# A gate read out of PSUM by ScalarE instead of VectorE, in a hybrid decoder step

## The chip, the cores and the metric

The kernel runs on one core of a Trainium2 chip. The metric is the device time of one launch in microseconds. The trace is one execution recorded by the hardware profiler; its times count from the first instruction. PE is TensorE's matmul row and PEld its weight loads, DVE is VectorE, ACT is ScalarE, POOL is GpSimd, and SP is the engine that issues most transfers. A tile is called by its name in the program.

## What is computed

One layer of a decoder with three branches that share one input projection, over a prompt of 1024 tokens and 8 single-token samples (1032 columns together, model width 1024):

```
h    = RMSNorm(x);  proj = h @ w_in          # split into 11 parts
A: dilated window attention, 12 heads of 64   * silu(z_A)   # 768 channels
B: u * (tril(W_s) @ LayerNorm(v) + b)         * silu(z_B)   # 512 channels
C: gated linear recurrence, 6 heads of 128    * silu(z_C)   # 768 channels, its q is silu(q_pre)
y    = x + concat(A, B, C) @ w_out
```

`silu(z) = z / (1 + exp(-z))`. The parts z_A, z_B, z_C and q_pre, 2816 channels in all, go through the function that is changed. All data are fp32; the large products are made of three passes over operands split into a high and a low part.

## The kernel before

`attention()` goes through three pairs of head pairs: projections of q, k, v and of z_A, then the attention of each head. `hgrn()` goes through three pairs of heads of branch C. For each pair it projects the values (`c_proj_i`, PSUM tile `pi`, and for the samples `pss_ci`). For each head it projects q and the forget gate (`c_proj_qf`, tile `pc`), runs the recurrence in chunks (`levels` and `c_head`: tiles `T` on DVE and ACT, products `lv`, `ls`, `po` on PE), the samples' step (`c_step`) and one head pair's attention of the samples over the cache (`decode`, with the small products `pmb` and `pda`, and `dmb` on DVE). Between the two heads stands the projection of z_C (`c_proj_z`, tile `pcz`). `sgu()` is branch B, with z_B in `pbz`. `out_proj` ends the program.

A transposed projection writes 128 channels by a third of the 1032 columns (344) at a time: 24 matmuls into one PSUM tile of tag `proj`, of which there are two. The tile is free again when its last reader is done. All projections, the natural ones too, take turns on these two tiles.

`gate(dst, ps, nm)` follows each such chunk of z or q. It runs 66 times: 18 for z_A, 18 for q, 18 for z_C, 12 for z_B. L152 reads PSUM on DVE and writes `max(ps, -43)` to `dst` in SBUF, L153 to L155 are three ACT instructions over the temporary `t`, and L156 multiplies on DVE. The temporary has tag `gt`, with two buffers; in `c_proj_qf` the forget gate's tile `ft` (written at L581 and last read at L582, both DVE) takes the same two buffers. The forget gate itself already goes from PSUM through ACT at L572, and L575 bounds its exponential in SBUF on DVE:

```
nc.scalar.activation(kk[:, cs], ps[:, :TC], AF.Exp, scale=-1.0)   # L572
nc.vector.tensor_scalar(kk, kk, 2.0 ** 62, None, ALU.min)         # L575
```

Weights come by transfer into `raw` tiles; ACT makes the high part (L192) and POOL the low part (L193) of each. The order of the instructions on each engine isn't written by hand: a planner (`schedule_with_timeline_sim=True`) takes the program's order as priority and its own table of costs, and lays the queues out. Each engine then works through its queue in order.

Of the kernel before, what the change touches and what calls it, by code (L numbers as in the profile page):

```python
# [12 lines left out]
AF = mybir.ActivationFunctionType  # L13
ALU = mybir.AluOpType
# [24 lines left out]
RUNS = ((0, 1, 3), (3, 3, 1), (4, 2, 2))  # L39
NEG = -3.0e38  # L40
BIG = 3.0e38
LIM = 43.0
N_BIG, N_S2, N_S2B, N_PQ, N_W, N_WL, N_GT, N_RAW, N_E = 16, 6, 2, 5, 4, 4, 2, 6, 3


# [46 lines left out]
def hybrid_step(tc, ins, outs, parts=("A", "D", "B", "C", "O"), dbg=None):  # L92
    nc = tc.nc
# [8 lines left out]
    with tc.tile_pool(name="const", bufs=1) as cp, tc.tile_pool(name="sb", bufs=1) as sb, \  # L102
# [20 lines left out]
        def small(nm, n, p=P, dt=F32, bufs=2, tag=None):  # L123
            return sb.tile([p, n], dt, tag=tag or f"sm{n}", name=nm, bufs=bufs)
# [10 lines left out]
        def p_st(nm):  # L135
            return psum("st", nm, 4)
# [12 lines left out]
        def gate(dst, ps, nm):  # L149

            t = small(nm, TC, tag="gt", bufs=N_GT)
            nc.vector.tensor_scalar(dst, ps, -LIM, None, ALU.max)  # L152
            nc.scalar.activation(t, dst, AF.Exp, scale=-1.0)  # L153
            nc.scalar.activation(t, t, AF.Ln, bias=1.0)
            nc.scalar.activation(t, t, AF.Exp, scale=-1.0)  # L155
            nc.vector.tensor_tensor(dst, dst, t, ALU.mult)  # L156
# [49 lines left out]
        for t in (0, NT, *range(1, NT)):  # L206
# [7 lines left out]
            if t == NT:  # L214
                nc.vector.tensor_tensor_reduce(out=xn[:n, :], in0=xt[:n, :], in1=xt[:n, :], op0=ALU.mult, op1=ALU.add,
                                               scale=1.0, scalar=0.0, accum_out=ss[:n, 0:1])
# [9 lines left out]
            for j in range(2):  # L226
                ps = p_st(f"tr0_{t}_{j}").rearrange("p (a b) -> p a b", a=4)
# [151 lines left out]
        def az_proj(sp):  # L379
            blk = load_w([(OFF_AZ + sp * NW, NW)], f"az{sp}")  # L380
            Z = [inp(f"az{sp}_{j}") for j in range(2)]
            for j in range(2):
                for c in range(3):
                    ps = p_proj(f"paz{sp}_{j}_{c}")
                    proj_T(blk, j * P, c, ps[:, :TC])
                    gate(Z[j][:, c * TC:(c + 1) * TC], ps[:, :TC], f"azt{sp}_{j}_{c}")
                nc.scalar.copy(ysT[:, 2 * sp + j, :], Z[j][:, S:L])
            return Z
# [172 lines left out]
        def c_proj_qf(h):  # L561
            blk = load_w([(OFF_CQ + h * P, P), (OFF_CF + h * P, P)], f"cqf{h}")
            f, q, kk = inp(f"f{h}"), inp(f"q{h}"), inp(f"k{h}")
            for j, dst in ((1, kk), (0, q)):
                for c in range(3):
                    ps = p_proj(f"pc{h}_{j}_{c}")
                    proj_T(blk, j * P, c, ps[:, :TC])
                    cs = slice(c * TC, (c + 1) * TC)
                    if j == 0:
                        gate(q[:, cs], ps[:, :TC], f"qt{h}_{c}")  # L570
                    else:
                        nc.scalar.activation(kk[:, cs], ps[:, :TC], AF.Exp, scale=-1.0)  # L572
                if j == 1:

                    nc.vector.tensor_scalar(kk, kk, 2.0 ** 62, None, ALU.min)  # L575
                    nc.scalar.activation(f, kk, AF.Ln, bias=1.0)
                    nc.scalar.activation(f, f, AF.Exp, scale=-1.0)
                    for c in range(3):
                        cs = slice(c * TC, (c + 1) * TC)
                        t = small(f"ft{h}_{c}", TC, tag="gt", bufs=N_GT)  # L580
                        nc.vector.scalar_tensor_tensor(t, kk[:, cs], 1.0, f[:, cs], ALU.add, ALU.mult)  # L581
                        nc.vector.scalar_tensor_tensor(f[:, cs], t, 2.0, f[:, cs], ALU.subtract, ALU.mult)  # L582
            nc.vector.scalar_tensor_tensor(kk, kk, lb1[:, h:h + 1], f, ALU.mult, ALU.mult)
            nc.scalar.activation(f, f, AF.Identity, scale=lb1[:, h:h + 1], bias=lb[:, h:h + 1])
            qw = small(f"qs{h}", 5 * NS, tag="qs", bufs=2)
            nc.gpsimd.memset(qw[:, 3 * NS:], 0.0)
            qs = qw[:, 0:3 * NS].rearrange("p (a b) -> p a b", a=3)
            for i, x in enumerate((q, f, kk)):
                nc.scalar.copy(qs[:, i, :], x[:, S:L])
            return q, f, kk, qw  # L590
# [14 lines left out]
        def c_proj_z(hp):  # L605
            blk = load_w([(OFF_CZ + hp * NW, NW)], f"cz{hp}")
            Z = [inp(f"cz{hp}_{j}") for j in range(2)]
            for j in range(2):
                for c in range(3):
                    ps = p_proj(f"pcz{hp}_{j}_{c}")  # L610
                    proj_T(blk, j * P, c, ps[:, :TC])
                    gate(Z[j][:, c * TC:(c + 1) * TC], ps[:, :TC], f"czt{hp}_{j}_{c}")
            for j in range(2):
                nc.scalar.copy(zsT[:, 2 * hp + j, :], Z[j][:, S:L])
            return Z
# [463 lines left out]
```

## Time and profile before

| | us |
|---|---|
| median of 3 runs | 1289.98 |
| lowest and highest of them | 1288.97, 1293.23 |
| the profiled execution, device time | 1287.74 |
| its span, first to last instruction | 1286.0 |
| what lies around the span | 1.74 |

The mean granted TensorE clock of the span is 0.977 of full speed. The stages, by the span: attention up to about 475, branch C from there to about 975 with the first projections of branch B inside its end, branch B to about 1065, and the output projection to the end. PE, DVE and ACT work on neighbouring stages at once, since the planner fills one stage's gaps with the next one's projections.

### The profile page before, as it was taken

The numbers are of one execution on the slowest core, as the hardware profiler recorded it, in microseconds if no ns is written. First come the engines' busy times: TensorE is split into PE (matmuls) and PEld (weight loads), VectorE is DVE, ScalarE is ACT, GpSimd is POOL, SyncE is SP. The second block draws the span as 40 slices with busy tenths as digits, with TensorE's granted clock in tenths as the row PEclk, the third lists the DMA queues.
The fourth block names the chain that finished last, engine by engine and source line by source line (L and its number), as shares of the span: only waits on it lengthen the run. The fifth ranks groups of instructions, "written<-read, shape, count | busy, mean of one in ns | idle before, by whom it ended". The sixth has DMA issues, their size and how long they took to land.

```text
span 1286.0 us, 27698 instructions
## 1 busy us (share of the span) xinstructions
PE 1215.2 (94%) x10610; PEld 1129.3 (88%) x10610; DVE 916.5 (71%) x2427; ACT 644.2 (50%) x1486; POOL 285.5 (22%) x272
## 2 busy tenths in 40 slices
PE   4899989999999999998999989997999999999998
PEld 3899979999899988997888878887889899899998
DVE  5844778668776685879888897889796534664643
ACT  4444444745347554565445554565443242454543
POOL 3532112312123121121011111111011254122221
PEclk9999989999899999999999989999899999999999
DMA  6151032312223123124343424424353224621110
GB/s 234 24 148 54 14 105 62 111 51 59 57 78 107 38 84 89 29 64 107 91 134 96 117 61 134 132 66 106 95 153 95 86 68 134 203 79 46 62 47 29
DMA packets 165045, 114.17 MB, mean 89 GB/s; under 512 B 13945, under 2 KB 158993, under 8 KB 164913
## 3 DMA queue, kind: packets, MB, share of 16 engines
q1 hardware_dynamic: 157520, 110.28, 29.4%
q10 hardware_dynamic: 6816, 1.54, 0.6%
q8 instruction: 83, 1.36, 0.5%
q0 software_dynamic: 576, 0.58, 0.3%
q14 instruction: 50, 0.40, 0.1%
HBM read 84.47 MB, written 22.09 MB: 83 GB/s over the span
## 4 chain that ended last, share of the span: by engine, by line
PE 75%; DVE 15%; DMA 4%; issue 3%; ACT 2%; SPq 0%; POOL 0%; ACTq 0%; DVEq 0%; POOLq 0%
PE po L100 15%; PE pqk L100 10%; PE pv L100 9%; PE paz L100 5%; PE pi L100 5%; PE st L100 4%; PE pbu L100 4%; PE pc L100 4%; PE pbz L100 4%; PE pbv L100 3%; PE pcz L100 2%; PE s L100 2%; DMA dk<-in_cache_k_dram 2%; DVE T L628 2%; DVE T L630 1%
## 5 line engine op out<-in xcount | busy, mean ns | idle before, releaser
L100 PE MATMUL pqk<-wh_qk,h 128*128 128x256 f32 x768 | 157.4, 294 | 5.8 <-ACT h L233 3.0
L100 PE MATMUL pc<-h,wh_cqf 128*128 128x344 f32 x576 | 141.6, 326 | 11.3 <-DVE cz L152 8.0
L100 PE MATMUL po<-woh,yh 128*128 128x256 f32 x512 | 144.1, 282 | 0.5 <-ACT yh L1027 0.5
L100 PE MATMUL po<-woh,yl 128*128 128x256 f32 x512 | 144.2, 282 | 0.0
L100 PE MATMUL po<-wol,yh 128*128 128x256 f32 x512 | 143.4, 280 | 0.0
L100 PEld LDWEIGHTS pqk<-wh_qk,h 128*128 128x128 f32 x768 | 127.8, 197 | 12.3 <-ACT h L233 4.3
L100 PE MATMUL pqk<-wl_qk,h 128*128 128x256 f32 x384 | 113.0, 294 | 0.0
L100 PEld LDWEIGHTS pc<-h,wh_cqf 128*128 128x128 f32 x576 | 100.4, 190 | 14.0 <-DVE cz L152 8.8
L100 PEld LDWEIGHTS po<-woh,yl 128*128 128x128 f32 x512 | 96.2, 188 | 3.0 <-issue 1.7
L100 PEld LDWEIGHTS po<-woh,yh 128*128 128x128 f32 x512 | 96.3, 188 | 2.3 <-ACT yh L1027 2.3
L100 PEld LDWEIGHTS po<-wol,yh 128*128 128x128 f32 x512 | 96.5, 188 | 0.0
L437 DVE CUSTOM_DVE_ANT_0 s<-s,masks 128x512 f32<-128x512 f32 (+2 forms) x144 | 77.6, 578 | 22.7 <-PE s L100 21.7
L100 PE MATMUL pc<-h,wl_cqf 128*128 128x344 f32 x288 | 93.7, 327 | 0.0
L100 PE MATMUL pi<-wh_ci,h 128*128 128x256 f32 x384 | 77.5, 295 | 0.8 <-DVE T L635 0.8
L100 PEld LDWEIGHTS pqk<-wl_qk,h 128*128 128x128 f32 x384 | 75.9, 198 | 1.8 <-issue 0.7
L100 PE MATMUL pv<-wh_v,h 128*128 128x256 f32 x384 | 75.3, 287 | 0.3 <-DVE ss L164 0.3
L100 PE MATMUL pcz<-h,wh_cz 128*128 128x344 f32 x288 | 72.2, 330 | 2.3 <-DVE q L152 2.3
L100 PE MATMUL paz<-h,wh_az 128*128 128x344 f32 x288 | 69.0, 323 | 0.0
L1028 DVE TENSOR_TENSOR yl<-yb,yh 128x512 fp32r<-128x512 f32 x44 | 30.3, 691 | 53.3 <-ACT yh L1027 53.3
L100 PEld LDWEIGHTS pi<-wh_ci,h 128*128 128x128 f32 x384 | 63.5, 198 | 2.7 <-issue 2.4
L100 PEld LDWEIGHTS pv<-wh_v,h 128*128 128x128 f32 x384 | 61.8, 193 | 1.9 <-issue 1.2
L1027 ACT CAST yh<-yb 128x512 fp32r<-128x512 f32 x64 | 39.6, 620 | 43.4 <-PE po L100 43.4
(379 smaller groups left out, 3581.6 us busy)
## 6 DMA issues: line engine op xcount, KB each, us to landing
wro<-in_w_out_dram SPq DMA_DIRECT2D x32, 256.0 KB
wr_qk<-in_w_in_dram SPq DMA_DIRECT2D x48, 128.0 KB
wr_cqf<-in_w_in_dram SPq DMA_DIRECT2D x48, 128.0 KB
dk<-in_cache_k_dram SPq DMA_DIRECT2D x24, 192.0 KB
dv<-in_cache_v_dram SPq DMA_DIRECT2D x24, 192.0 KB
xt<-in_x_prompt_dram SPq DMA_DIRECT2D x8, 512.0 KB
xr<-in_x_prompt_dram SPq DMA_DIRECT2D x32, 128.0 KB
out_o_yp_dram<-xr SPq DMA_DIRECT2D x32, 128.0 KB
```

What stands on the lines that cost most here:

```text
L100: nc.tensor.matmul(out, lhsT=lhsT, rhs=rhs, start=start, stop=stop)
L437: nc.vector.tensor_tensor_reduce(out=ps[:, :w], in0=ps[:, :w], in1=nmask[:, S - n + c:S - n + c + w], op0=ALU.add, op1=ALU.max, scale=1.0, ...
L628: nc.vector.tensor_tensor(K.rearrange("p (n w) -> p n w", w=w), g3[:, :, w - 1:w].to_broadcast([P, 4 * n, w]), h3, ALU.subtract)
L630: nc.vector.tensor_tensor(Q[:, 0:3], g4[:, 1:4], g4[:, 0:3, :, w - 1:w].to_broadcast([P, 3, n, w]), ALU.subtract)
L1027: nc.scalar.copy(yh[:, sl, :], y)
L1028: (nc.gpsimd if piece == 0 else nc.vector).tensor_tensor(yl[:, sl, :], y, yh[:, sl, :].bitcast(F32), ALU.subtract)
```

## The change

The gate no longer reads PSUM on DVE. ACT takes the exponential of the negated argument straight from PSUM into the temporary, and copies the unbounded argument from PSUM to `dst`. DVE bounds the exponential in SBUF at 2 to the power 62, in place. The logarithm, the second exponential and the product stay. The function is called at the same four places, 66 times.

```diff
@@ -39,7 +39,6 @@
 BIG = 3.0e38
-LIM = 43.0
 N_BIG, N_S2, N_S2B, N_PQ, N_W, N_WL, N_GT, N_RAW, N_E = 16, 6, 2, 5, 4, 4, 2, 6, 3
@@ -149,8 +148,9 @@
             t = small(nm, TC, tag="gt", bufs=N_GT)
-            nc.vector.tensor_scalar(dst, ps, -LIM, None, ALU.max)
-            nc.scalar.activation(t, dst, AF.Exp, scale=-1.0)
+            nc.scalar.activation(t, ps, AF.Exp, scale=-1.0)
+            nc.scalar.copy(dst, ps)
+            nc.vector.tensor_scalar(t, t, 2.0 ** 62, None, ALU.min)
             nc.scalar.activation(t, t, AF.Ln, bias=1.0)
             nc.scalar.activation(t, t, AF.Exp, scale=-1.0)
             nc.vector.tensor_tensor(dst, dst, t, ALU.mult)
```

## Rows read from the trace of the kernel before

**Rows 1.** The page, part 1: busy us (share of the span) and instructions of each engine.
```profile
PE 1215.2 (94%) x10610; PEld 1129.3 (88%) x10610; DVE 916.5 (71%) x2427; ACT 644.2 (50%) x1486; POOL 285.5 (22%) x272
```

**Rows 2.** The page, part 4: the chain that ended last, share of the span by engine.
```profile
PE 75%; DVE 15%; DMA 4%; issue 3%; ACT 2%; SPq 0%; POOL 0%; ACTq 0%; DVEq 0%; POOLq 0%
```

**Rows 3.** Windows: length, then each engine's busy us (instructions), granted clock, DMA share, GB/s.
```profile
247.00:278.00 31.00, 31.00 (x211) 29.32 (x210) 18.98 (x51) 20.10 (x44) 14.44 (x18) 1.00 0.33 97
...
530.00:975.00 445.00, 413.82 (x4355) 378.39 (x4354) 382.88 (x1076) 238.63 (x564) 73.68 (x68) 0.97 0.37 102
...
975.00:1065.00 90.00, 90.00 (x746) 83.52 (x745) 48.93 (x136) 34.84 (x80) 30.64 (x24) 1.00 0.30 90
...
755.00:760.00 5.00, 3.76 (x25) 2.27 (x18) 4.94 (x16) 4.38 (x9) 1.49 (x1) 0.50 0.48 138
```

**Rows 4.** Waits of PE from 530 to 975: us in total, times, longest.
```profile
PE pc L100 <- DVE cz L152: 8.0, 3, 3.0
...
PE pss_ci L100 <- DVE q L152: 4.3, 2, 3.7
...
PE pss_bv L100 <- DVE q L152: 3.7, 1, 3.7
...
PE pcz L100 <- DVE q L152: 2.3, 2, 1.8
...
PE pc L100 <- DVE q L152: 0.9, 2, 0.5
...
PE pc L100 <- ACT V L602: 2.5, 2, 2.2
...
PE pmb L941 <- DVE dmb L939: 5.0, 3, 3.4
```

**Rows 5.** Instructions of four lines: duration in ns (min/median/max), first and last start.
```profile
L152 DVE TENSOR_SCALAR q<-pc x18: 496/501/517, 532.8 to 900.2; 128x344 f32<-128x344 f32 x18
...
L572 ACT ACTIVATE k<-pc x18: 444/458/461, 512.5 to 879.2; 128x344 f32<-128x344 f32 x18
...
L575 DVE TENSOR_SCALAR k<-k x6: 682/687/699, 524.9 to 882.7; 128x1032 f32<-128x1032 f32 x6
...
L939 DVE COPY dmb<-dmb x6: 207/215/1199, 612.8 to 960.3; 16x128 f32<-16x128 f32 x6
```

**Rows 6.** Timeline, 742 to 758: start, duration (us), what [idle before <-releaser].
```profile
742.66 0.51 DVE L152 TENSOR_SCALAR q<-pc 128x344 f32<-128x344 f32 x1
...
745.45 0.49 ACT L153 ACTIVATE qt<-q 128x344 f32<-128x344 f32 x1 [2.39 <-DVE f L582]
...
754.27 0.50 DVE L152 TENSOR_SCALAR q<-pc 128x344 f32<-128x344 f32 x1
...
754.81 0.49 ACT L153 ACTIVATE qt<-q 128x344 f32<-128x344 f32 x1 [2.91 <-DVE q L152]
...
754.83 1.89 PE L100 MATMUL pss_ci<-wr_ci,hs 128*8 128x256 f32 x16 [3.68 <-DVE q L152]
...
755.88 1.49 POOL L193 TENSOR_TENSOR wl_ci<-wr_ci,wh_ci 128x512 fp32r<-128x512 f32 x1 [1.75 <-ACT wh_ci L192]
...
756.25 1.20 DVE L939 COPY dmb<-dmb 16x128 f32<-16x128 f32 x1
...
757.50 0.29 PE L941 MATMUL pmb<-ident,dmb 16*128 16x16 f32 x1 [0.78 <-DVE dmb L939]
```

**Rows 7.** Timeline, 606 to 609.
```profile
606.36 6.45 POOL L193 TENSOR_TENSOR wl_ci<-wr_ci,wh_ci 128x512 fp32r<-128x512 f32 x4 [27.47 <-ACT wh_ci L192]
...
608.05 0.50 DVE L152 TENSOR_SCALAR q<-pc 128x344 f32<-128x344 f32 x1
```

**Rows 8.** Timeline of PE, 727 to 732.
```profile
727.39 0.58 PE L100 MATMUL pc<-h,wh_cqf 128*128 128x344 f32 x2 [3.02 <-DVE cz L152]
...
731.59 0.25 PE L100 MATMUL lv<-T 128*32 128x32 f32 x2
```

**Rows 9.** Window 530 to 975, line L193 alone: POOL busy us (instructions), then clock and DMA.
```profile
530.00:975.00 445.00, 70.84 (x51) 0.97 0.37 102
```

## The prediction

> **What bounds the kernel now.** I first read the page's busy times: PE is busy 94% of the span, DVE 71%, ACT 50% [rows 1]. The chain of waits is three quarters PE and 15% DVE, and only 2% ACT [rows 2]. So the kernel is bound by PE, and a change on DVE and ACT can move the end only through PE's idle time. The windows say where that is. Beside the gates of z_A and z_B, PE is busy in all of 31.00 us and in all of 90.00 us. In the stage of branch C it is busy for 413.8 of 445 us, so it idles for 31.2 us, while DVE is busy for 86% of that stage and ACT for 54% [rows 3]. Next I read PE's waits in this stage: five rows name L152, the gate's reading of PSUM on DVE. They sum to 8.0 + 4.3 + 3.7 + 2.3 + 0.9 = 19.2 us [rows 4]. In these PE waits for one of the two projection tiles, because DVE is late in emptying it. Where ACT empties the tile, PE waited 2.5 us in all.
>
> One such place shows how it comes about. ACT idles 2.91 us and PE 3.68 us for the same L152, which stands at 754.27 in a full DVE queue [rows 6]; in 755 to 760 DVE is busy 4.94 of 5 us and the granted clock after the gap is 0.50, the level of 1.2 GHz [rows 3]. Then PE waits again, for `dmb`, which also comes from DVE [rows 6].
>
> **The change part by part.** It issues no transfer, and moves none past another: only three instructions of each gate change. Of 66 gates, the 30 of z_A and z_B I cost at nothing: the cover is PE's unbroken work there [rows 3], against which ACT's addition is small. If that cover were gone, 30 copies of 0.46 us would cost 13.7 us. What follows is for the 36 gates of branch C.
>
> *DVE's work.* A maximum from PSUM of 0.501 us goes, and a minimum in SBUF comes. L575 is the same operation on 1032 columns, 0.687 us; a copy in SBUF of 128 columns takes 0.215 [rows 5]. The line between them gives 0.33 us at 344 columns; 0.215 and 0.501 bound it. So 0.17 us is saved each, 36 x 0.17 = 6.2 us. That counts only where DVE is late. I take half, -3.1 us, since DVE is full around the waits and 86% busy over the stage; the bounds are 0 and -6.2 (-10.3 at 0.215).
>
> *PSUM released by ACT.* The tile is free after exponential and copy instead of after L152. ACT idles where PE waits [rows 6], so it can be there first, and up to 19.2 us can go. But PE works in order, and behind each wait stands a product that needs DVE too. The 3.02 us wait at 727.39 is followed at 731.59 by `lv`, which reads `T` from DVE [rows 8]. If PE starts 3 us sooner it may stand there instead. For the rows of `pc` and `pcz`, 11.2 us, I take half, -5.6 us, the share for which projection work can still be done before the next DVE result. For `pss_ci` and `pss_bv`, 8.0 us, I take only -1.0: the next but one instruction is `pmb` [rows 6], so what is won is waited for at `dmb`, less the shorter DVE queue. The bounds are 0 and -19.2. What the clock would give back I put at nothing, for the gap at 751 to 757 stays; if it closed, that comes on top.
>
> *ACT's work.* The copy of 128x344 from PSUM isn't in the trace. The nearest row is the exponential of the same shape from PSUM, 0.458 us [rows 5]; I take it. 36 x 0.46 = 16.5 us. The gate's exponential itself falls from 0.49 [rows 6] to this 0.46, -1.1 us. So the bounds are -1.1 and +16.5. I take +2.0, near the low end, as ACT is a small part of the chain and has nearly half of the stage free. Behind the copy in ACT's queue stand the exponentials of `T`, for which DVE and then PE wait.
>
> *A new wait.* The logarithm now waits for DVE's minimum, as the first exponential waited for L152. The number of such waits on ACT is the same, but they no longer hold PSUM of the same gate. They can hold the next gate's, behind them in ACT's queue.
>
> *GpSimd beside the minimum.* A copy in SBUF on DVE takes 1.20 us where L193 runs beside it on POOL, and 0.215 elsewhere [rows 5, 6]; L152, which reads PSUM, takes 0.50 in the middle of 6.45 us of L193 [rows 7]. So the new operation can be held where the old one was not. L193 covers 70.84 of 445 us, 16% [rows 9]; 36 x 0.16 = 5.7 minimums by 0.98 us each are 5.6 us of DVE time. I take half as with DVE's saving, +2.8. The bounds are 0 and, if all 36 met it, +35.
>
> The Trainium skill, SBUF — State Buffer, section Who interferes with whom, says that a copy or scalar operation of DVE in its two-port mode and a GpSimd instruction exclude each other, the later one standing still until the other ends, while an operation with at most one SBUF input outside those modes doesn't contend. By that rule each minimum that meets L193 is held, as the 1.20 us of this trace agrees, and the full 5.6 us would be paid instead of 2.8: the sum would be -2.1 instead of -4.9.
>
> *Sum.* -3.1 - 5.6 - 1.0 + 2.0 + 2.8 = -4.9 us. The profiled execution took 1287.74 us, so 1282.8; the median of the runs is 2.2 us above it, and against that it is 1289.98 - 4.9 = 1285.1. I predict 1285 us.
>
> **The rivals.**
>
> *The waits only move.* PE stands at `lv`, `pmb` and `po` for as long as it stood at L152. For it speaks that DVE is full where PE waits [rows 3]; against it, that ACT's own releases cost PE 2.5 us in all [rows 4]. Without the two PSUM terms the sum is +1.7, and the time 1291.7.
>
> *GpSimd holds the minimum.* The minimums fall together with L193 as often as its share says, and each such microsecond counts. The copy of 1.20 us speaks for it [rows 6], the 16% against [rows 9]. With +5.6 in place of +2.8 the time is 1287.9.
>
> *All of PE's wait goes.* The planner puts enough projection work behind each released tile. For it speaks that ACT was idle at the very place [rows 6]; against it, `pmb` behind it. -19.2 - 3.1, with nothing paid on ACT or for GpSimd, gives 1267.7.
>
> *The temporaries hold PSUM: slower.* L152 needed no temporary; it freed PSUM at once. Now the first reader of PSUM writes `t`, of which there are two, shared with `ft`. At 742.66 L152 freed the first chunk of q by 743.17, while the exponential waited 2.39 us for L582 to give up a temporary and began at 745.45 [rows 6]. With exponential and copy behind that wait PSUM is free at 745.45 + 0.46 + 0.46 = 746.4, 3.2 us later. Where PE needs the tile in this time it idles. All six heads would pay 6 x 3.2 = 19.2 us; three of them pay 9.6, and the PSUM term keeps only the z_C half (-4.0). Then -3.1 - 4.0 + 2.0 + 2.8 + 9.6 = +7.3, 1297.3; with six heads 1307. Against it: the other chunks of q gain at the same time, and the second tile gives PE a chunk's time of grace. It decides once PE's new waits for the gate's copy pass some 9 us.
>
> That the planner lays out all queues of the stage anew, since the costs change, adds to every case a few microseconds of either sign.
>
> **How the numbers follow.** The forecast has 0.40, from 1280 to 1289 by its own terms; the moved waits 0.17, GpSimd 0.10, all of the wait 0.12, the temporaries 0.21. Less than 0.3%, 3.9 us, can't be told from no change. Faster: 0.34 of the forecast and 0.12 of the third rival, 0.46. Same: 0.06 of the forecast, 0.14 of the moved waits, 0.09 of GpSimd, 0.01 of the last: 0.30. Slower: 0.20 of the temporaries, 0.03 and 0.01 of the first two: 0.24. The range is 1273 to 1298: it leaves out half of the third rival's cases below and the dearer half of the last one's above, some 2 in 10.
>
> **What would show it.** Right: PE's rows that name L152 are gone or below 3 us from 530 to 975, PE's idle time there is near 26 us, the minimum takes 0.33 us at the median, the copy 0.46, and the windows beside z_A and z_B stay full. The waits moved: rows of PE for `dmb`, `cmat` or `T` grow by as much as those of L152 fall. GpSimd: minimums near 1.2 us, more than six. The temporaries: PE waits for the gate's copy on ACT, and the gate's exponential for L582 or L156. Wrong beyond that: a stage outside 530 to 975 that changes by more than 2 us.

## The result, and the profile after

| | us |
|---|---|
| after, median (lowest to highest) | 1311.19 (1308.36 to 1312.36) |
| before, median of the same comparison | 1290.84 |
| ratio of after to before | 1.0169, 95% interval 1.0145 to 1.0193 |
| profiled execution of after, its span | 1311.43, 1309.7 |

The change makes the kernel 1.7% slower, some 20 us. The prediction was 1285 us, range 1273 to 1298, 0.24 for slower. In the listing of the kernel after, called after from here on, the gate is L151 (exponential), L152 (copy), L153 (minimum) to L156; the helper of the products is L99.

The page's busy times after:

```profile
PE 1227.9 (94%) x10610; PEld 1134.6 (87%) x10610; DVE 912.1 (70%) x2427; ACT 663.7 (51%) x1552; POOL 312.6 (24%) x272
```

Beside [rows 1], DVE has lost 4 us, ACT has gained 20, POOL has gained 27, though no instruction of POOL was touched, and PE has gained 13: more time busy for the same 10610 products. PE's idle time, span less busy, rose from 70.8 to 81.8 us.

The windows of [rows 3], after:

```profile
247.00:278.00 31.00, 31.00 (x208) 29.12 (x207) 19.02 (x54) 21.58 (x50) 14.96 (x19) 1.00 0.35 105
530.00:975.00 445.00, 406.85 (x4276) 371.21 (x4275) 371.26 (x1068) 245.29 (x594) 96.56 (x65) 0.96 0.36 101
975.00:1065.00 90.00, 86.90 (x715) 81.32 (x715) 48.49 (x141) 29.34 (x72) 20.46 (x16) 0.96 0.25 74
```

PE idles 38.2 us in branch C's stage where it idled 31.2, and there is now a gap in the stage of branch B, where there was none.

The waits of PE from 530 to 975, after (us, times, longest), beside [rows 4]:

```profile
PE pc L99 <- POOL wl_cqf L193: 9.6, 5, 3.5
PE pmx L936 <- DVE dmx L934: 7.7, 2, 5.0
PE pc L99 <- POOL qs L586: 3.5, 1, 3.5
...
PE pi L99 <- ACT q L152: 1.3, 2, 0.8
```

The gate's rows, 19.2 us, are down to 1.3 (and two of 0.3). In their place stand rows that were not there: the weights' low part (`wl_cqf`) and a memset (`qs`) from POOL, and `dmx`, the maximum in the decode, from DVE.

Durations in branch C, after (ns, min/median/max; first and last start):

```profile
L153 DVE TENSOR_SCALAR qt<-qt x18: 320/331/1345, 536.8 to 909.8; 128x344 f32<-128x344 f32 x18
...
L152 ACT COPY q<-pc x18: 426/441/455, 535.0 to 906.0; 128x344 f32<-128x344 f32 x18
...
L193 POOL TENSOR_TENSOR wl_cqf<-wr_cqf,wh_cqf x24: 1254/1312/5658, 505.9 to 876.9; 128x512 fp32r<-128x512 f32 x24
```

The two durations were as forecast: the minimum 0.33 us, the copy 0.44. The sign was wrong all the same, and the traces differ in more than these operations: before, the low parts of head 1's four blocks were made at 572.35, 574.65 and 576.10 (two in 2.79 us); after, three of them in one run from 579.02:

```profile
579.02 9.24 POOL L193 TENSOR_TENSOR wl_cqf<-wr_cqf,wh_cqf 128x512 fp32r<-128x512 f32 x3 [1.96 <-ACT wh_cqf L192]
```

That is 9.24 us for three where two took 2.79. The planner has laid out every engine's queue anew.

### The profile page after: what moved, and what is told of

The parts are those of the page before. It is cut to its first block, busy times and chain, and to the rows that moved or that the text cites. A ratio compares the mean times of both kernels' runs of the same rounds, so it can differ in the third digit from the quotient of the medians.

```text
span 1309.7 us, 27776 instructions
## 1 busy us (share of the span) xinstructions
PE 1227.9 (94%) x10610; PEld 1134.6 (87%) x10610; DVE 912.1 (70%) x2427; ACT 663.7 (51%) x1552; POOL 312.6 (24%) x272
## 5 line engine op out<-in xcount | busy, mean ns | idle before, releaser
L99 PE MATMUL pqk<-wh_qk,h 128*128 128x256 f32 x768 | 152.3, 290 | 5.2 <-DVE ss L164 2.0
L99 PE MATMUL pc<-h,wh_cqf 128*128 128x344 f32 x576 | 146.6, 337 | 1.0 <-ACT wh_cqf L192 0.7
L99 PE MATMUL po<-woh,yh 128*128 128x256 f32 x512 | 144.9, 283 | 0.0
L99 PE MATMUL po<-woh,yl 128*128 128x256 f32 x512 | 144.2, 282 | 0.0
L99 PE MATMUL po<-wol,yh 128*128 128x256 f32 x512 | 144.0, 281 | 0.0
L99 PEld LDWEIGHTS pqk<-wh_qk,h 128*128 128x128 f32 x768 | 125.3, 195 | 10.0 <-ACT h L233 2.2
L99 PE MATMUL pqk<-wl_qk,h 128*128 128x256 f32 x384 | 111.4, 290 | 0.0
L99 PE MATMUL pc<-h,wl_cqf 128*128 128x344 f32 x288 | 98.2, 344 | 13.2 <-POOL wl_cqf L193 9.6
L99 PEld LDWEIGHTS pc<-h,wh_cqf 128*128 128x128 f32 x576 | 105.6, 200 | 2.9 <-ACT wh_cqf L192 1.0
L99 PEld LDWEIGHTS po<-woh,yh 128*128 128x128 f32 x512 | 96.2, 188 | 6.0 <-ACT yh L1027 4.3
L99 PEld LDWEIGHTS po<-woh,yl 128*128 128x128 f32 x512 | 96.6, 189 | 2.6 <-issue 1.3
L99 PEld LDWEIGHTS po<-wol,yh 128*128 128x128 f32 x512 | 96.4, 188 | 0.0
L99 PE MATMUL pv<-wh_v,h 128*128 128x256 f32 x384 | 76.2, 291 | 1.6 <-DVE sd_v L260 1.3
L99 PEld LDWEIGHTS pqk<-wl_qk,h 128*128 128x128 f32 x384 | 74.8, 195 | 1.4 <-issue 0.2
L193 POOL TENSOR_TENSOR wl_cqf<-wr_cqf,wh_cqf 128x512 fp32r<-128x512 f32 x24 | 49.7, 2095 | 109.6 <-ACT wh_cqf L192 109.6
L99 PE MATMUL pi<-wh_ci,h 128*128 128x256 f32 x384 | 73.0, 287 | 2.8 <-DVE sd_ci L260 1.5
L99 PE MATMUL pcz<-h,wh_cz 128*128 128x344 f32 x288 | 71.7, 329 | 0.0
L99 PEld LDWEIGHTS pc<-h,wl_cqf 128*128 128x128 f32 x288 | 57.2, 199 | 16.7 <-POOL wl_cqf L193 11.4
L99 PE MATMUL paz<-h,wh_az 128*128 128x344 f32 x288 | 69.4, 323 | 0.0
L99 PEld LDWEIGHTS pv<-wh_v,h 128*128 128x128 f32 x384 | 62.5, 194 | 4.1 <-issue 1.4
```

The costliest lines, as they stand in the source:

```text
L99: nc.tensor.matmul(out, lhsT=lhsT, rhs=rhs, start=start, stop=stop)
L193: nc.gpsimd.tensor_tensor(lo, raw, hi.bitcast(F32), ALU.subtract)
```

## The experiments

Two theories. **Order**: the planner's new order of all the other instructions costs the time. **Operations**: what is done in the gate costs it (minimum against GpSimd, copy on ACT, temporaries).

**Operations and order apart.** Four kernels, each gate under each order. The program is planned once with one gate and the order of all instructions outside the gates is noted for each engine; then it is built with either gate, and these instructions are tied, each to the one before it on its engine. The gate's own instructions the planner places freely.

```diff
+    _, order = build(ORDER_NEW, None)
+    nc, got = build(OPS_NEW, order)
...
+                for seq in order.values():
+                    for a, b in zip(seq, seq[1:]):
+                        tc.add_manual_dep(rest[b], rest[a].name, mybir.DependencyInfo(
+                            mybir.DependencyClass.NoSync, mybir.DependencyReason.DATA), reason="order")
```

Old gate, old order: 

> The control: the gate of before, and on every engine all instructions outside the gate tied to the order that the planner gave them in the kernel before; the gate's own instructions the planner places freely. Both theories: as before, ratio 0.997 to 1.003, 1290 us. If it is not, the tying itself changes the time and the other three runs are read against this one.

New gate, old order: 

> The gate of after, all instructions outside it tied to the order of before. Theory that the new order costs the time: the operations themselves do what the prediction summed, so ratio 0.992 to 1.003 to before, 1280 to 1294 us; PE's waits for the gate's first reader of PSUM in branch C fall from 19 us to below 5. Theory that the operations cost it (the minimum against GpSimd's subtraction, the copy in ACT's queue, the temporaries): 1.012 to 1.02, 1305 to 1316 us, as after.

Old gate, new order: 

> The gate of before, all instructions outside it tied to the order that the planner gave them with the gate of after. Theory that the new order costs the time: 1.010 to 1.02, 1303 to 1316 us, with the long waits of PE and DVE for the cache's transfers (dk) after 900 us as in the profile after, 16 us of DVE in place of 5. Theory that the operations cost it: 0.997 to 1.005, 1286 to 1296 us.

New gate, new order: 

> The second control: the gate of after under the order of after, tied in the same way. Both theories: as after, 1.014 to 1.019, 1308 to 1315 us.

| ratio to before (95% interval) | order of before | order of after |
|---|---|---|
| gate of before | 1.0010 (0.9990 to 1.0030) | 1.0131 (1.0095 to 1.0168) |
| gate of after | 1.0019 (1.0001 to 1.0037) | 1.0180 (1.0147 to 1.0213) |

The columns differ by 1.2 and 1.6%, the rows by 0.1 and 0.5%. The order costs the time, some 16 to 21 us (by the intervals 10 to 26), and does so with the old gate too; the 0.5% between the gates under the new order is no larger than its interval (the long waits of DVE for `dk` that were expected with it weren't there: 1.0 us after 880). The operations under the old order come to about +1 us against the tied control (by the intervals -2 to +5). PE's waits from 530 to 975 under the old order, old gate and then new (the tied kernels have seven more lines: L158 is the old gate's maximum, L155 the new one's copy):

```profile
PE pc L100 <- DVE cz L158: 7.9, 3, 3.0
PE pmb L948 <- DVE dmb L946: 5.0, 3, 3.4
PE pss_ci L100 <- DVE q L158: 3.8, 2, 3.2
...
PE pss_bv L100 <- DVE q L158: 2.8, 1, 2.8
PE pcz L100 <- DVE q L158: 2.2, 2, 1.8
```

```profile
PE pmb L948 <- DVE dmb L946: 7.9, 3, 4.6
PE lv L100 <- DVE T L641: 6.0, 3, 2.6
PE pc L100 <- POOL qs L593: 3.5, 1, 3.5
PE pc L100 <- POOL wl_cqf L200: 3.3, 1, 3.3
...
PE pcz L100 <- ACT q L155: 1.7, 2, 1.1
```

This is the change without the re-planning, and it reads as the rival that the waits only move: 17.5 us of waits for the gate (with a row of 0.8 not shown) become 1.7, and PE stands instead at `lv`, `pmb`, `qs` and `wl_cqf`. Its busy time in this stage goes from 415.25 to 416.08 of 445 us.

**The minimum alone.** The same kernel, new gate in the old order, without the gate's third line: the bound of the exponential is left out.

```diff
-                nc.vector.tensor_scalar(t, t, 2.0 ** 62, None, ALU.min)
```

> The gate of after without DVE's minimum: the bound of the exponential is left out. All other instructions tied to the order of before, as in the run with the minimum (1.0019). Theory that the minimum and GpSimd hold each other on the path (the prediction's +2.8 at half): 1.9 to 6 us less than with it, 0.997 to 1.000. Rival that DVE's work isn't what PE waits for: within 1.5 us of it, 1.001 to 1.003.

Measured 0.9959 (0.9938 to 0.9980), 1284.46 us. With the minimum it was 1.0019 (1.0001 to 1.0037): 0.6%, 7.7 us (by the intervals 4 to 11), where the theories gave 1.9 to 6 and under 1.5. The page's busy times with it and without it:

```profile
PE 1217.1 (95%) x10610; PEld 1131.9 (88%) x10610; DVE 906.7 (70%) x2427; ACT 663.8 (52%) x1552; POOL 300.6 (23%) x272
```

```profile
PE 1213.9 (95%) x10610; PEld 1129.6 (88%) x10610; DVE 886.1 (69%) x2361; ACT 658.1 (51%) x1552; POOL 296.9 (23%) x272
```

DVE is relieved of 20.6 us, and 7.7 us are won at the end, so the minimum does count. The row that was to show GpSimd held by it does not change: POOL's slowest `wl_cqf` takes 6.33 us with it and 6.52 without, and only three of the 36 minimums of branch C are held beside POOL (1.41 to 1.42 us). So the theory that the two hold each other *on the path* is not borne out. What is not separated is DVE's time from the link in the gate's chain: without the minimum ACT's logarithm follows its exponential directly, and with it ACT waits 17.5 us for DVE's minimum, half of it in q's gates:

```profile
ACT qt L160 <- DVE qt L156: 8.8, 6, 1.8
```

**Where in the order it is lost.** The gate of after everywhere; all other instructions follow one order up to a given gate and the other order behind it.

```diff
+    done = set(head[:cut])
+    order = queues(head[:cut] + [i for i in tail if i not in done], engine)
```

New order first, to 611 us: 

> The gate of after everywhere. All other instructions tied: the order of after up to the gate of the third chunk of q of the first pair's second head (about 611 us), behind it the remaining instructions in the order of before. Theory that the order costs its time at a few places which can be told apart: the 12 us that the two tied runs of this gate lie apart at that point stay and the rest of the 21 us goes, 1299 to 1306 us, 1.007 to 1.014 to before. Theory that an order costs by the way in which its whole fits: not near the sum, either below 1295 or above 1308.

Old first, to 611 us: 

> The other half: the order of before up to the same gate, behind it the remaining instructions in the order of after. Places: the first 12 us go and the 5 us about 970 us and the 5 us of the last stage stay, 1297 to 1304 us, 1.005 to 1.012 to before. Whole: not near it.

Old first, to 898 us: 

> The gate of after everywhere. All other instructions tied: the order of before up to the gate of the last head's third chunk of q (about 898 us), behind it the remaining instructions in the order of after. With the cut at 611 us this side of the order gave 1.0154. Theory that the end of branch C and what follows holds the cost (idle of PE from 900 to 1065 rose by 8 us there): 1.009 to 1.016, 1300 to 1309 us. Theory that it comes from 611 to 900 us: 1.000 to 1.005, 1288 to 1295 us.

Old first, to 987 us: 

> As the two cuts before: the gate of after everywhere, the order of before up to the first gate of z_B (about 987 us), behind it the order of after. With the cut at 898 us it was 1.0118, with the order of before to the end 1.0019. Theory that the last head's recurrence beside the last pair's decode (898 to 987 us) holds most of the 13 us: 1.002 to 1.006, 1290 to 1296 us. Theory that the stages behind it hold it (the output projection ended 9 us later than the recurrence did): 1.007 to 1.012.

Old first, to 1009 us: 

> As the cut at 987 us (1.0119), now at the gate of the last chunk of the first half of z_B (about 1009 us); behind it PE has no long wait in either order. Between the two cuts lie the transposes of the mixing weights (wtp, rs), where PE idled 6.9 us and ran at a clock of 0.83 for 20 us. Theory that this place and the order of the output's products hold about half each: 1.004 to 1.008, 1294 to 1300 us. Theory that only waits cost: 1.001 to 1.003. Theory that the order of the output's products holds nearly all: 1.010 to 1.012.

| order | ratio to before (95% interval) |
|---|---|
| new to 611, then old | 1.0019 (1.0000 to 1.0038) |
| old to 611, then new | 1.0154 (1.0124 to 1.0185) |
| old to 898, then new | 1.0118 (1.0079 to 1.0158) |
| old to 987, then new | 1.0119 (1.0095 to 1.0142) |
| old to 1009, then new | 1.0049 (1.0030 to 1.0069) |
| old to the end | 1.0019 (1.0001 to 1.0037) |

By what was expected the first two rows speak against the theory of places (1.007 to 1.014 and 1.005 to 1.012) and for its rival: 1293.44 us lies below 1295, 1308.93 not near 1297 to 1304. With the new order to 611 us, three low parts in 9.25 us on POOL included, nothing is lost at the end (by the intervals 3 us either way). The copy of the third chunk of q at which this cut lies comes 12 us later than in the old order (623.4 and 611.7 us), the next head's only 4 us later (686.1 and 682.1): the delay isn't kept, and PE's 29 us of waits in branch C are room in which it can be made up.

The other rows price the new order from a gate on, with the old order ahead of it: 0.7%, 9 us, hang on whether it begins at 987 or at 1009 (the first theory had put most of the cost into the recurrence before 987; its rival's 1.007 to 1.012 came), and about 0.3%, 4 us, on what stands behind 1009. Whether it begins at 898 or at 987 makes no difference that shows (by the intervals 6 us either way); from 611 to 898 it is 0.3%, which the intervals don't separate from nothing either. So some 13 of the 21 us are placed.

Windows 980 to 1000, old order to the end, and then with the cut at 987 us:

```profile
980.00:1000.00 20.00, 20.00 (x174) 19.46 (x168) 18.02 (x82) 8.78 (x30) 0.00 (x0) 1.00 0.31 91
```

```profile
980.00:1000.00 20.00, 13.07 (x105) 9.97 (x103) 18.34 (x78) 3.80 (x16) 0.00 (x0) 0.83 0.29 82
```

PE goes from no gap to 6.93 us of idle time, and the granted clock from 1.00 to 0.83, so part of the stretch runs at the level of 1.2 GHz, the lower of the clock's two (2.4 GHz is the other). PE's timeline there with the cut, then the same products in the old order:

```profile
988.12 0.39 PE L100 MATMUL pns<-ssq,ones 128*128 128x48 f32 x2 [0.86 <-DVE dmx L965]
990.03 0.66 PE L807 MATMUL wtp<-ident,wn 128*128 128x128 f32 x4 [1.52 <-ACT ssq L792]
993.22 1.11 PE L807 MATMUL wtp<-ident,wn 128*128 128x128 f32 x4 [2.53 <-DVE wn L809]
996.35 1.97 PE L100 MATMUL rs<-wn,ones 128*64 128x512 f32 x4 [2.02 <-DVE wn L809]
```

```profile
992.26 0.32 PE L100 MATMUL pns<-ssq,ones 128*128 128x48 f32 x2
...
995.96 0.38 PE L807 MATMUL wtp<-ident,wn 128*128 128x128 f32 x2
997.07 0.38 PE L807 MATMUL wtp<-ident,wn 128*128 128x128 f32 x2
1001.78 0.60 PE L807 MATMUL wtp<-ident,wn 128*128 128x128 f32 x4
1006.87 1.08 PE L100 MATMUL rs<-wn,ones 128*64 128x512 f32 x4
```

These are the transposes of branch B's mixing weights: PE transposes four, DVE masks them (`wn`, L809), PE goes on. The old order spreads them over 15 us with projection work in between; the new one puts them one behind the other, and PE pays each answer. The four waits shown, 0.86, 1.52, 2.53 and 2.02 us, are the whole 6.93.

After itself loses less at this place and more ahead of it. Windows of after, then with the cut at 987 us:

```profile
900.00:987.00 87.00, 77.84 (x919) 70.22 (x919) 75.62 (x245) 40.38 (x104) 16.35 (x12) 0.96 0.35 99
987.00:1009.00 22.00, 18.90 (x227) 16.72 (x227) 17.95 (x65) 6.01 (x16) 2.64 (x3) 0.84 0.41 115
```

```profile
900.00:987.00 87.00, 84.09 (x1059) 76.19 (x1058) 70.11 (x235) 36.65 (x89) 13.54 (x13) 0.96 0.43 124
987.00:1009.00 22.00, 15.07 (x82) 11.99 (x81) 17.32 (x70) 7.51 (x26) 0.00 (x0) 0.84 0.06 19
```

PE idles 9.2 and 3.1 us in after, 2.9 and 6.9 with this cut (old order to the end: 2.7 and 0). With the cut at 898 us it idles 10.0 and 2.6, as in after, and the time is that of the cut at 987. So the old order up to 987 spares PE 7 us of waits, 5.6 of them for `dmx`, and behind 987 about as much is lost as they cost. The 9 us belong to the whole stretch from 900 to 1009; that they come from chains which are no longer interleaved is read from the traces, and no run put only these chains back.

Behind 1009 PE's idle time does not grow; over the whole span its busy time does, from 1217.1 us in the old order to 1223.6 with this cut. What differs are the samples' products of the output projection (`pon`, `pos`, all that read the tile `ysT` there). PE's busy time in them, old order to the end, and then with the cut at 1009 us:

```profile
980.00:1310.00 330.00, 12.31 (x160) 1.00 0.25 79
```

```profile
980.00:1310.00 330.00, 17.03 (x160) 1.00 0.25 79
```

The same 160 products cover 17.03 us instead of 12.31: 4.7 us, about the 4 us that this part costs. They are pipelined, so how long they cover depends on what stands beside them, which the last section shows. After has 17.03 too.

**One wait moved.** In the order with the cut at 898 us PE's longest wait from 900 on is 5.6 us for `dmx`, DVE having idled 2.2 us for a transfer of `dk` before it. In that order the decode's instructions on DVE were moved behind the running chain, and `pmx` and `pmb` later on PE.

```diff
+        mine = [i for i in order[e] if i in part["decode2"]]
+        if e.endswith("DVE"):
+            order[e] = move(order[e], mine[6:15], mine[15])
+        if e.endswith("PE"):
+            later = order[e][order[e].index(mine[1]) + 20]
+            order[e] = move(move(order[e], mine[0:1], mine[1]), mine[1:2], later)
```

> The cut at 898 us (1.0118) with one thing moved in the order behind it: in the last pair's decode, the second half of the samples' cache products on DVE, their maximum and what follows it stand behind the running chain of the recurrence instead of in the middle of it, and on PE the transposes pmx and pmb stand so many instructions later. Theory that the wait of PE for the maximum dmx (5.6 us, with DVE idle 2.2 us for the transfer of dk just before) is one of the places that cost: 4 to 7 us less, 1.006 to 1.009. Rival that what is won there is waited for at the next product: 1.010 to 1.013.

Measured 1.0125 (1.0102 to 1.0149), as without the move (1.0118); the wait fell from 5.6 to 3.8 us. A wait shorter by 1.8 us can't be told from nothing here (by the intervals 6 us either way), so this run alone doesn't decide. The cuts say more: with the cut at 987 the wait is gone, and the time is the same.

**Other orders.** The exponential and the copy exchanged, nothing tied:

```diff
-            nc.scalar.activation(t, ps, AF.Exp, scale=-1.0)
             nc.scalar.copy(dst, ps)
+            nc.scalar.activation(t, ps, AF.Exp, scale=-1.0)
```

> The kernel after with two lines of the gate changed about: the copy stands ahead of the exponential in the program. The work is the same, and nothing is tied; the planner lays the queues out from this program. Theory that a new order moves the time whatever the work is: a time of its own between 1285 and 1320 us, more than 4 us from after (1311). Theory that what is done in the gate sets it: 1307 to 1315 us.

The new gate for branch C only, then for z_A and z_B only (the other calls go to the old gate under the name `gate_max`):

> The gate of after for q and z_C only (36 of 66), the gate of before for z_A and z_B; nothing is tied. Theory that what is done in branch C costs the time: 1305 to 1315 us, as after. Theory that a new order moves the time whatever the work is: anywhere from 1285 to 1320 us, and its PE waits in branch C are at other places than those of after.

> The gate of after for z_A and z_B only (30 of 66), the gate of before for q and z_C; nothing is tied. By the prediction's pricing these 30 cost nothing, and PE is busy without a gap beside them. Theory that the operations set the time: 0.998 to 1.003, 1287 to 1293 us. Theory that a new order moves the time whatever the work is: 1.005 to 1.02, with PE's new waits in branch C, where no gate is changed.

The old gate, with each z_C projection's chunks last to first:

```diff
-                for c in range(3):
+                for c in (2, 1, 0):
```

> The kernel before with the three chunks of each z_C projection written last to first; the same instructions with the gate of before, nothing tied; the planner lays the queues out from this program. Theory that the order of before is an uncommonly good one and others of the same work lie above it: 1.004 to 1.02, 1293 to 1315 us. Theory that orders of the old gate all lie close together and only the new gate draws worse ones: 0.997 to 1.004, 1286 to 1294 us.

The kernel after without the minimum (the bound is left out), nothing tied:

> The kernel after without the minimum (the bound of the exponential is left out), nothing tied. In the order of before this gate gave 0.9959. Theory that every order that is laid out anew for ACT's reading costs 0.8 to 1.5%: 1.004 to 1.011. Theory that the planner's order is good or bad from case to case, as the third gate's was as good as that of before: 0.994 to 1.003.

| nothing tied | minimum in the program | ratio (95% interval) |
|---|---|---|
| after | 66 | 1.0169 (1.0145 to 1.0193) |
| copy first | 66 | 1.0125 (1.0086 to 1.0163) |
| branch C only | 36 | 1.0150 (1.0123 to 1.0178) |
| z_A, z_B only | 30 | 1.0064 (1.0041 to 1.0087) |
| old gate, chunks reversed | none | 1.0014 (0.9992 to 1.0036) |
| after without minimum | none | 0.9981 (0.9967 to 0.9994) |

That any new order costs 1% is refuted by the last two rows (the chunks reversed change little of the order; without the minimum it is laid out anew as in after, the samples' products covering 17.20 us). The four orders planned with the minimum are all dearer, so after did not draw a single bad one, as far as four related programs can tell; part of the gap is the minimum's own price, 0.6% in the old order. With branch C alone PE's waits there are those of after (9.9 us for `wl_cqf`, 7.7 for `dmx`), against the expectation that a new order puts them elsewhere. With z_A and z_B alone PE's waits in branch C are again those of the old gate (8.0, 5.8 and 3.4 us for `cz`, `dmb`, `q`), and PE's windows beside z_A and z_B stay full. Of its 0.6%, 8 us, the samples' products take 3.3 (15.61 us); the rest is open. Whether the copy's place matters can't be told: its interval overlaps that of after.

**A gate without the minimum that still bounds.** ACT reads PSUM once, with a Relu that bounds at -20; the exponential's bias gives the 20 back.

```diff
-            nc.scalar.activation(t, ps, AF.Exp, scale=-1.0)
-            nc.scalar.copy(dst, ps)
-            nc.vector.tensor_scalar(t, t, 2.0 ** 62, None, ALU.min)
+            nc.scalar.activation(dst, ps, AF.Relu, bias=bound)
+            nc.scalar.activation(t, dst, AF.Exp, scale=-1.0, bias=bound)
...
-            nc.vector.tensor_tensor(dst, dst, t, ALU.mult)
+            nc.vector.scalar_tensor_tensor(dst, dst, BOUND, t, ALU.subtract, ALU.mult)
```

Tied to the old order: 

> A third gate: ACT alone reads PSUM, once (Relu of the argument plus 20 into SBUF, which bounds it at -20), the exponential takes the 20 back through its bias, and DVE only multiplies, subtracting 20 in the same instruction; no minimum. All other instructions tied to the order of before. Without the minimum the gate of after gave 0.9959 in that order; this one frees PSUM after one ACT instruction instead of two and has the same work on DVE. Expected: 0.992 to 0.998, 1279 to 1287 us, below both kernels. Theory that DVE's work doesn't count: 1.000 to 1.004.

Nothing tied: 

> The same third gate, nothing tied; the planner lays the queues out from this program. If every new order costs 10 to 20 us beside the one of before, as with the gate of after, then 0.995 plus 0.008 to 0.015, so 1.003 to 1.01. If the order's cost belongs to the gate of after, 0.992 to 1.000.

Measured 0.9995 (0.9975 to 1.0014) tied, which misses the expected 0.992 to 0.998, and 1.0010 (0.9994 to 1.0025) untied: 1.6% below after and no better than before. So no kernel here computes the whole gate faster than before; only those without the bound do. Untied, its samples' products cover 17.63 us, so the dear layout of the output projection is no mark of the minimum. In the old order it is above the gate with no bound (0.9959), though DVE has as much to do (886.8 and 886.1 us). ACT has 20 us more, 678.5 against 658.1, and PE's wait for `dmb` is 9.7 us against 5.8. That ACT's 20 us are the reason fits, but was not tried apart.

## Why the prediction was wrong

**The step that failed is its last term**, that the planner's new layout "adds to every case a few microseconds of either sign". It was left out of the sum and had no rival and no share of the chances, and it measured +16 us with the old gate and +21 with the new one. Everything else together was -4.9 us. [rows 3] showed PE busy in all of 90.00 us from 975 on. I read that as cover for z_B's gates; it was itself a product of the order, which set projection work between the transposes and DVE's answers, and the new order lost it (86.90). The prediction's own sign for "wrong beyond that", a stage outside 530 to 975 that changes by more than 2 us, came true there.

**The sum of the operations** was -4.9 us and measured about +1 in the old order (1.0019 against the control's 1.0010, by the intervals -2 to +5 us). Within it:

- *PSUM released by ACT, -6.6.* The mechanism was right: PE's waits for the gate fell to 1.7 us. The share was wrong: nearly all of it was waited for elsewhere, at `lv` and `pmb`, as the first rival had it, and at `qs` and `wl_cqf` from POOL, which it had not. That rival's +1.7 us is close to the 1.0019, +2.4 us, of this kernel.
- *DVE's work, -3.1.* DVE's page time fell by 10.2 us in the old order. Leaving out the minimum took 20.6 us from DVE and 7.7 from the time, 0.4 for each, near the half that was taken; but it also takes a link out of the gate's chain.
- *GpSimd beside the minimum, +2.8.* After's 36 minimums of branch C took 18.8 us in all, 6.8 above 36 times 0.333; eight of them took 0.76 to 1.41 us. That is near the forecast of 5.7 held ones and 5.6 us. In the old order only three were held. By the Trainium skill's rule (SBUF — State Buffer, Who interferes with whom), as the prediction drew on it, each that meets L193 is held; the trace does not agree: 13 met it, and five of these took 0.32 to 0.33 us (in the old order 11 met it, and eight were not held). So DVE paid about the GpSimd rival's price in after, but that isn't what made the kernel slow.
- *z_A and z_B at nothing.* z_A's window stayed full, as predicted; it is one stretch of several, and from 100 to 475 us PE idled 8.0 us after and 7.4 before. z_B's did not stay full. The program in which only these 30 gates are new is 0.6% slower, so the term is wrong as a forecast for a program that is planned anew.
- *ACT's work, +2.0.* The copy's duration was right (0.44 for 0.46); its cost at the end was not measured apart. The new gate without the minimum, copy included, is 0.5% below the old gate in the same order.

**The rivals.** Temporaries holding PSUM would have given the right sign for a reason that did not occur: the gate's rows of PE's waits are 1.9 us in after where 9 was the point that decides. "All of PE's wait goes" fell with the waits that moved.

What stays open: why the planner lays out a dearer order when a DVE instruction stands between two of ACT's in the gate. No run looked into its decisions. Some 8 of the order's 21 us are not placed either.

## What to carry to other kernels

Where a planner orders the queues, a change has two effects, and they can be measured apart: tie everything outside the edit to the old order, and the edit's own price shows (here 0.1%, with 1.6% for the order). In a forecast the re-planning needs its own term, and the place to look for its price is where engines are full by interleaving, far from the edit as well as at it. A long wait or a delay in the trace is no evidence of a loss of that size: 12 us of delay at 611 were made up, and an order without the 5.6 us wait for `dmx` was no faster, since the chains of PE and DVE behind it then stood without projection work between them.

## What the runs showed of the hardware

*A change between small and large products is dear.* PE in the order of before, and with the cut at 1009 us:

```profile
1088.43 1.05 PE L100 MATMUL pon<-wro,ysT 128*8 128x256 f32 x16
...
1089.76 0.28 PE L100 MATMUL po<-wol,yh 128*128 128x256 f32 x1
1089.88 0.28 PE L100 MATMUL po<-woh,yl 128*128 128x256 f32 x1
```

```profile
1090.05 0.38 PE L100 MATMUL po<-woh,yh 128*128 128x256 f32 x1
1090.27 0.28 PE L100 MATMUL po<-wol,yh 128*128 128x256 f32 x1
1090.48 0.39 PE L100 MATMUL pon<-wro,ysT 128*8 128x256 f32 x2
...
1090.70 0.39 PE L100 MATMUL pon<-wro,ysT 128*8 128x256 f32 x2
```

Sixteen products over 8 columns in a row take 1.05 us, 0.07 each; products over 128 columns follow each other every 0.12. The step from the first large product to the second takes 0.22 us, and that from the last large one to the first small one 0.21. (From 1090.48 to 1090.70 start four small ones, of which two are shown.) In the trace the 160 small products stand in 11 runs in the old order and in 21 with the cut: 4.7 us for ten more runs, some 0.5 us each, an estimate. The kernel writes the small products to four groups of 32 partitions (`rows8`). The Trainium skill (TensorEngine Tiling (Array Packing), section Key Properties) says that changing the tiling mode drains the engine; the longer steps at each change agree, and it gives no price.

*GpSimd starves behind a dense run of DVE.* L193 took up to 5.66 us where 1.31 is its median, while DVE, in the kernel after, went on like this from 581.36 to 584.44:

```profile
581.62 0.41 DVE L628 TENSOR_TENSOR T<-G,H 128x256 f32<-128x256 f32 x1
581.96 0.35 DVE L630 TENSOR_TENSOR T<-G 128x192 f32<-128x192 f32 x1
582.23 0.28 DVE L640 TENSOR_TENSOR T_q<-f,q 128x128 f32<-128x128 f32 x1
...
585.58 0.33 DVE L153 TENSOR_SCALAR czt<-czt 128x344 f32<-128x344 f32 x1
```

DVE's operations go on at 0.28 to 0.41 us each; POOL's three subtractions stretch. In [rows 6] it was DVE's copy that took 1.20 us beside L193. The Trainium skill (SBUF — State Buffer, Who interferes with whom) says that a DVE operation with two SBUF inputs contends with a GpSimd instruction that reads SBUF; the 9.24 us agree, and here the one that lost stood through many of the other's instructions.

*A minimum beside L193 is held or not.* The minimum at 585.58, inside the same stretch of POOL, took 0.33 us; another, inside a shorter stretch of L193, took four times as long:

```profile
731.69 1.41 DVE L153 TENSOR_SCALAR czt<-czt 128x344 f32<-128x344 f32 x1
```

*A bias held in a tile costs ACT 0.09 us.* The exponential of 128x344 from SBUF took 0.580 us with it in the third gate, the second exponential, without it, 0.488. The Trainium skill (ScalarE: Activation LUTs, What ACT_TABLE_LOAD costs) gives about 93 ns for each such operand, and this agrees.
